# Decay gates as one stacked product, tokens that begin at 128 bytes, and mixing in the wide PSUM bank

## The chip, the cores and the metric

The kernel runs on one core of one Trainium2 chip. Its time is the device time of one execution in microseconds (us); the median of several runs counts. A profile shows one execution, taken by the hardware profiler. Engines: TensorE (PE; its weight loads PEld), VectorE (DVE), ScalarE (ACT), GpSimd (POOL) and SyncE (SP), which issues the DMAs.

## The reference

One block of a streaming encoder on 1024 tokens and 16 meta tokens in front of them, width 1024, all in float32. A normed input is projected into eight parts. One branch takes trailing means over 2, 4, 8 and 16 positions and mixes them; the other is gated linear attention in chunks of 64, whose decays come from a product of rank 16; both are merged by gates. A squared-ReLU MLP of width 4096 follows. Cut to what the change touches:

```python
z = jnp.einsum('bld,dn->bln', u, w_in)
a, q, k, v, r, lr, ga, gb = jnp.split(z, IN_SPLITS, axis=-1)     # lr: 16 columns
p = multiscale_pool(a).reshape(B, L, POOL_GROUPS, POOL_GROUP_DIM)
p = jnp.einsum('blgc,gce->blge', p, w_pool_mix).reshape(B, L, POOL_WIDTH) * pool_scale
...
log_a = jax.nn.log_sigmoid((lr @ w_gate_up + b_gate).astype(jnp.float32)) / GLA_TAU
...
o = gla_chunked(q, k, v, log_a)
```

## The kernel before

Nearly every matrix product is made from operands split in two: `hi` is the value rounded to float32r by a ScalarE copy, `lo` the rest by a VectorE subtraction, and a product is three float32r matmuls, hi·hi + hi·lo + lo·hi (`mm3`, lines 280 to 282). The tokens live transposed, features on the partitions, in four tiles: `TH[0]`, `TL[0]` for the first 512 tokens and `TH[1]`, `TL[1]` for the rest, each with 8 blocks (k) of 128 features. The first half's rows hold 528 numbers: the 16 meta tokens, then the 512 tokens, which so begin at number 16, or byte 64 (`OFF`, line 208). The second half's rows hold 512.

The stages, in the order of TensorE's program:

- `start` (line 431): for each tile of 128 tokens the norm, the transposes into `TH`/`TL` (`transposed`, lines 266, 222, 223), and the value projections with the tokens as the stationary operand (`v_tile`, line 390). The first group's value weights carry 16 more columns, the rank-16 input `lr` (272 columns in place of 256). At its end `lr_turn` (line 412) transposes `lr` into `lrT_meta` and into the first 16 partitions of `gB`, by nine transposes and three ScalarE copies. The gate weights `wgu` (16 rows of 256) are loaded there as well (line 502).
- Pooling, gates and keys: `pool_open` (line 539) gives the room of `start` back and makes the buffers; then the steps of the list in line 631 follow: four pooling blocks `a_block`, two decay steps `decays`, four mixing steps `mix_block`, and the two key blocks `k_block`, in the order a0, gate 0, a1, gate 1, mix 0, a2, mix 1, a3, mix 2, k0, mix 3, differences, k1. A pooling or key block projects all 1040 tokens in three pieces (`WITH_META`, line 285): 264 + 264 columns of the first half with the meta tokens, and 512 of the second; 24 matmuls each.
- A decay step (`log_decay`, line 511) makes two products of 512 tokens and one of the 16 meta tokens, each as one float32 matmul over 16 rows with `wgu` as weights (line 514); then a chain of five ScalarE and one VectorE instructions makes log-sigmoid and the decay of each half (lines 515 to 519, 528).
- A mixing step (line 568) makes the window sums on VectorE, splits them into `ph`, and multiplies each half by the group's mixing weights. Before, the first half's product goes to a bank of the pool `ms`, which the gates and transposes use too, and the second half's to `sc`, one tile of two banks whose halves `bank("sc")` gives out in turn (line 154).
- The pairs of projections (line 764): the other projections as 11 pairs of blocks, each by seven products of half size. Products P1 and P2 (bank `sc`) take `TH[0]`/`TL[0]` as the moving operand, P5 and P3 (bank `z`) `TH[1]`/`TL[1]`, and P6, P7, P4 (bank `y`) sums of tokens in tiles of their own. Each product is a group of twelve matmuls of 512 columns. The attention inside the chunks is interleaved.
- Attention across the chunks, output projection, and the MLP by the same seven products. There P1 and P2 read `TH[0]`/`TL[0]` through views with rows of 512 numbers from the tile's beginning (`MH`, `ML`, line 210).

TensorE's order is the program's. The instructions of the other engines and the DMAs, which SyncE issues, are put in order by the scheduler from their dependencies and a cost model, and each engine works off its list in order. Weights come through two staging buffers (`Raw`) and the ring `W1` of two slots, split at lines 84 and 85. Storage on chip is two stacks, `left` and `right`; a tile pushed where another lay waits for that one's last use.

Of the kernel before, what the change touches and what calls it, by code (L numbers as in the profile page):

```python
# [7 lines left out]
F32 = mybir.dt.float32  # L8
# [19 lines left out]
C_A, C_Q, C_K, C_V, C_R, C_LR, C_GA, C_GB = 0, 512, 768, 1024, 1536, 2048, 2064, 3088  # L28
VP = 272
NPAIR = DFF // P // 2  # L30
MP = 264
PACE, LEVEL, OPENING, STRETCH = 1.3, 1.6, 6.0, 1.9


# [88 lines left out]
def kernel(  # L123
# [71 lines left out]
    stat = [tiny(16) for _ in range(4)]  # L195
    eps_t = tiny(1)
    pool.memset(eps_t, EPS)
    wgu = left.push("wgu", [16, 256], F32)
    metab = left.push("metab", [P, 5, 16], F32)
    lrT_meta = left.push("lrT_meta", [16, META], F32)  # L200
    raw = Raw(nc, [left.push(f"raw{i}", [P, D], F32) for i in range(2)])
    W1 = Ring(tc, raw, left.push("w1h", [P, 2, D], F32R), left.push("w1l", [P, 2, D], F32R), 2)
    left_ff = left.mark()
    TH, TL = [], []
    for h, n in ((0, HALF + META), (1, HALF)):
        TH.append(left.push(f"th{h}", [P, KT, n], F32R))
        TL.append(left.push(f"tl{h}", [P, KT, n], F32R))
    OFF = (META, 0)

    MH, ML = ([a.rearrange("p k c -> p (k c)")[:, : KT * HALF].rearrange("p (k c) -> p k c", k=KT) for a in t] for t in (TH, TL))  # L210

# [69 lines left out]
            pe.matmul(ps, ah, bl, start=False, stop=False, skip_group_check=more)  # L281
            pe.matmul(ps, al, bh, start=False, stop=last and i == n - 1, skip_group_check=more)  # L282

    MAIN = [(0, META, HALF), (1, 0, HALF)]
    WITH_META = [(0, 0, MP), (0, MP, MP), (1, 0, HALF)]

    def project(wb, pieces, evac, kt=KT, free=True, src=None):
        xh, xl = src or (TH, TL)
# [101 lines left out]
    def v_tile(i, t):  # L390

        vw, w = S["vw"][i], 256 + 16 * (i == 0)
        if t == 8:
            half, at, n = 0, 0, META
        else:
            half, n = t // 4, P
            at = OFF[half] + (t % 4) * P
        b = bank("mm")[:n, :w]
        mm3(
            b, KT, lambda k: (TH[half][:, k, at : at + n], TL[half][:, k, at : at + n]),  # L400
            lambda k: (vw[:, 0, k], vw[:, 1, k]),
        )
        if i == 0:
            dve.tensor_copy(S["lrtok"][:n, t], b[:, 256:])
        if t == 8:
            act.activation(vm[:, i * 256 : i * 256 + 256], b[:, :256], ACT.Copy)
        else:
            o = nxt("vo")
            act.activation(o, b[:, :256], ACT.Copy)
            nc.sync.dma_start(v_dram[i, t], o)  # L410

    def lr_turn():
        b = bank("ms")
        pe.transpose(b[:16, :16], S["lrtok"][:16, 8], ident[:16, :16])
        act.activation(lrT_meta, b[:16, :16], ACT.Copy)
        for h in range(2):
            b = bank("ms")
            for t in range(4):
                pe.transpose(b[:16, t * P : (t + 1) * P], S["lrtok"][:, 4 * h + t], ident)
            act.activation(gB[:16, h * HALF : (h + 1) * HALF], b[:16], ACT.Copy)  # L420


    SPREAD = {
# [7 lines left out]
    def start():  # L431
        act.preload_act_table_set("natural_log_exp_and_others")
        xs = left.push("xs", [P, 4, D], F32)
        us = left.push("us", [P, 3, D], F32)
        S["lrtok"] = left.push("lrtok", [P, 10, 16], F32)
        S["lrraw"] = left.push("lrraw", [P, KT, 16], F32)
        xm = left.push("xm", [META, D], F32)
        um = left.push("um", [META, D], F32)
        mf = left.push("mf", [P, 6, CH], F32)
        S["xr"] = right.push("xr", [P, KT, SEQ], F32)  # L440
        S["vw"] = [right.push(f"vw{i}", [P, 2, KT, n], F32R) for i, n in enumerate((VP, 256))]
        buffer("vo", 3, 2 * P, right)
        load = lambda t: nc.sync.dma_start(xs[:, t % 4], x[t * P : (t + 1) * P, :])
        blank = S["xr"].rearrange("p k c -> p (k c)")[:, -640:]
        pool.memset(blank, 0.0)

        def warm(n, cols=HALF):
            for _ in range(n):
                pe.matmul(bank("ms")[:, :cols], blank[:, HALF:], blank[:, :cols], start=True, stop=True)

        load(0)
        nc.sync.dma_start(um[:1], norm_mix[None, :])
        nc.sync.dma_start(ident, ident_in)
        ask_vw(0)
        nc.sync.dma_start(S["lrraw"], w_in[:, C_LR : C_LR + 16].rearrange("(k p) c -> p k c", p=P))
        pool.memset(xm[:1, :P], 1.0)
        warm(2)
        for c in halves():
            b = bank("mm")
            pe.matmul(b, xm[:1, :P], um[:1, c], start=True, stop=True)  # L460
            dve.tensor_copy(gB[:, c], b)
        warm(2)
        for t in range(8):
            if 0 < t < 6:
                load(t + 2)
            if t == 1:
                nc.sync.dma_start(xm, meta)
            if t == 3:
                W1.top_up()
            u = us[:, t % 3]  # L470
            layer_norm(xs[:, t % 4], u)
            transposed(u, t // 4, OFF[t // 4] + (t % 4) * P, ("ms", "sc"))
            if t == 0:
                load(1)
                load(2)
                warm(10, P)
                load_vw(0)
                ask_vw(1)
            if t == 6:
                layer_norm(xm, um)  # L480
            if t == 1:
                warm(6, P)
            if t == 2:
                load_vw(1)
            if t < 3:
                v_tile(0, t)
            else:
                for i, n in SPREAD[t]:
                    v_tile(i, n)
        transposed(um, 0, 0)  # L490
        v_tile(0, 7)
        v_tile(1, 6)
        v_tile(1, 7)
        v_tile(0, 8)
        v_tile(1, 8)
        lr_turn()
        nc.sync.dma_start(mf, masks)
        pool.tensor_copy(mask, mf)
        nc.sync.dma_start(pscale, col(pool_scale, 4))
        nc.sync.dma_start(bgate, col(b_gate, 2))  # L500
        nc.sync.dma_start(gnorm, col(gla_norm, 4))
        nc.sync.dma_start(wgu, w_gate_up)

    one = []
    step(one, start)
# [5 lines left out]
    def log_decay(lrT, p, n, y, t):  # L511

        b = bank("ms")[:, :n]
        pe.matmul(b, wgu[:, p * P : (p + 1) * P], lrT, start=True, stop=True)
        act.activation(y, b, ACT.Identity, bias=bgate[:, p : p + 1])
        act.activation(t, y, ACT.Abs)
        act.activation(t, t, ACT.Exp, scale=-1.0)
        act.activation(t, t, ACT.Ln, bias=1.0)
        dve.scalar_tensor_tensor(y, y, 0.0, t, ALU.min, ALU.subtract)
# [3 lines left out]
    def decays(p):  # L523
        def fn():
            for half, c in enumerate(halves()):
                y = nxt("c")
                log_decay(gB[:16, c], p, HALF, y, nxt("t1"))
                act.activation(y, y, ACT.Exp, scale=1.0 / TAU)
                nc.sync.dma_start(decay_dram[p, half], y)
                yield 0.6  # L530
            if p:
                act.activation(gnorm, gnorm, ACT.Copy, scale=0.5)
            log_decay(lrT_meta, p, META, metab[:, META_LOG[p]], metab[:, 4])
            if p:
                tc.keep_in_program_order(act.preload_act_table_set("exp_and_others"))

        return fn

    def pool_open():
        left.pop_to(base)  # L540
        right.pop_to(1)
        buffer("c", 4)
        buffer("t1", 3)
        S["left_t"] = left.mark()
        buffer("a", 2, 1056)
        buffer("s", 2, 1056)
        S["ph"] = left.push("ph", [P, 2, SEQ], F32R)
        mw = S["mw"] = left.push("mw", [P, 2, 4, P], F32R)
        r = raw.load(w_pool_mix.rearrange("g c e -> c g e"), 4 * P).rearrange("p (g e) -> p g e", g=4)
        act.activation(mw[:, 0], r, ACT.Copy)  # L550
        dve.tensor_tensor(mw[:, 1], r, f32(mw[:, 0]), ALU.subtract)
# [5 lines left out]
    def a_block(g):  # L557
        def fn(wb):
            a = pooled[g] = nxt("a")

            def evac(b, half, at, n):
                c = at if half == 0 else META + HALF
                act.activation(a[:, c : c + n], b, ACT.Copy)

            yield from project(wb, WITH_META, evac)

        return fn

    def mix_block(g):
        def fn():  # L570
# [10 lines left out]
            for c in halves():  # L581
                act.activation(S["ph"][:, 0, c], pp[:, c], ACT.Copy)
                dve.tensor_tensor(S["ph"][:, 1, c], pp[:, c], f32(S["ph"][:, 0, c]), ALU.subtract)
            for h, (tag, c) in enumerate(zip(("ms", "sc"), halves())):
                b = bank(tag)
                mm3(b, 1, lambda i: wb, lambda i: (S["ph"][:, 0, c], S["ph"][:, 1, c]))
                o = nxt("c")
                act.activation(o, b, ACT.Copy, scale=pscale[:, g : g + 1])
                nc.sync.dma_start(pm_dram[g, h], o)
                yield  # L590
# [3 lines left out]
    def k_block(p):  # L594
        def evac(b, half, at, n):
            o = nxt("c")[:, :n]
            act.activation(o, b, ACT.Copy)
            c = at if half == 0 else META + HALF
            nc.sync.dma_start(k_dram[p, :, c : c + n], o)

        return lambda wb: project(wb, WITH_META, evac)
# [1029 lines left out]
```

## Time and profile before

| | |
|---|---|
| median of 3 runs | 1226.18 us |
| the runs | 1226.18, 1223.92, 1226.18 us |
| profiled execution | 1222.42 us |
| its span, first to last instruction | 1220.6 us |
| mean granted TensorE clock | 0.999 |
| matmuls in the span | 6807 |

In the rows of a timeline stand start and length in us, the engine, the line, the operation and `out<-in` with shapes and a count; instructions of one kind that follow each other are merged into one row. A bracket at the end is the engine's idle time before the row and who ended it. In the table of stages stand the stretch, its length, and then for each engine its busy time with the number of instructions, in the order PE, PEld, DVE, ACT, POOL; then the granted clock, the share of the DMA engines and GB/s.

### The profile page before, as it was taken

What the parts mean: (1) busy time and instruction counts of PE and PEld (TensorE: products, weight loads), DVE (VectorE), ACT (ScalarE), POOL (GpSimd) and SP (SyncE); (2) the same over time, 40 slices, a digit from 0 to 9 for tenths busy, and PEclk for the clock granted to TensorE, in tenths of its full rate; (3) what the DMA queues carried; (4) which work ended last, traced back from release to release, by engine and by line L of the source; (5) the groups of instructions that cost most, each with busy time, mean ns of one, the idle gap of its engine ahead of it and who ended that gap; (6) DMA issues with size and microseconds to landing.
All of it is one profiled execution on the core that took longest, in us unless ns stands there. A gap on an engine that the chain in (4) does not pass through costs nothing.

```text
span 1220.6 us, 18363 instructions
## 1 busy us (share of the span) xinstructions
PE 1204.6 (99%) x6807; PEld 996.5 (82%) x6807; DVE 838.9 (69%) x1381; ACT 572.3 (47%) x1009; POOL 75.7 (6%) x96
## 2 busy tenths in 40 slices
PE   9999999999999999999999999999999999999997
PEld 7988977777778887888778888888888888888886
DVE  7536557565777569735887677676775887887686
ACT  8536444444456224314655455454554444444544
POOL 0000053322230000000000000000000000000000
PEclk9999999999999999999999999999999999999999
DMA  8213334435338967821244454444569973333532
GB/s 261 73 35 114 104 95 137 141 104 166 96 121 291 326 222 248 296 67 69 104 139 156 143 162 152 148 155 145 173 228 322 334 246 104 96 95 96 171 96 87
DMA packets 153355, 192.76 MB, mean 158 GB/s; under 512 B 12177, under 2 KB 88225, under 8 KB 153266
## 3 DMA queue, kind: packets, MB, share of 16 engines
q1 hardware_dynamic: 153266, 191.59, 48.9%
q8 instruction: 53, 0.87, 0.3%
q14 instruction: 36, 0.29, 0.1%
HBM read 128.62 MB, written 62.93 MB: 157 GB/s over the span
## 4 chain that ended last, share of the span: by engine, by line
PE 89%; DVE 4%; DMA 3%; ACT 1%; issue 1%; POOL 0%; SPq 0%; DVEq 0%; ACTq 0%; POOLq 0%
PE b_mm L280 7%; PE b_mm L282 7%; PE b_mm L281 7%; PE b_y L280 6%; PE b_y L282 6%; PE b_y L281 6%; PE b_oa L281 5%; PE b_oa L282 5%; PE b_oa L280 5%; PE b_z L280 4%; PE b_z L282 4%; PE b_z L281 4%; PE b_sc L280 4%; PE b_ob L281 4%; PE b_ob L282 4%; PE b_ob L280 4%
## 5 line engine op out<-in xcount | busy, mean ns | idle before, releaser
L685 ACT ACTIVATE w1h<-raw 128x512 fp32r<-128x512 f32 x106 | 65.9, 623 | 57.9 <-PE b_y L281 25.3
L686 DVE TENSOR_TENSOR w1l<-raw,w1h 128x512 fp32r<-128x512 f32 x106 | 72.5, 685 | 20.5 <-ACT w1h L685 20.5
L280 PE MATMUL b_sc<-th,w1h 128*128 128x512 f32 x216 | 85.7, 397 | 0.7 <-ACT u2p L1414 0.7
L280 PE MATMUL b_z<-th,w1h 128*128 128x512 f32 x216 | 85.3, 395 | 0.6 <-DVE c L804 0.4
L281 PE MATMUL b_sc<-tl,w1h 128*128 128x512 f32 x216 | 84.9, 393 | 0.0
L281 PE MATMUL b_z<-tl,w1h 128*128 128x512 f32 x216 | 84.3, 391 | 0.4 <-DVE tl L1300 0.4
L282 PE MATMUL b_sc<-th,w1l 128*128 128x512 f32 x216 | 84.5, 391 | 0.0
L685 ACT ACTIVATE w1h<-fs 128x512 fp32r<-128x512 f32 x81 | 51.1, 631 | 71.1 <-PE b_y L281 33.2
L282 PE MATMUL b_z<-th,w1l 128*128 128x512 f32 x216 | 84.2, 390 | 0.0
L686 DVE TENSOR_TENSOR w1l<-fs,w1h 128x512 fp32r<-128x512 f32 x81 | 56.9, 702 | 25.9 <-ACT w1h L685 25.8
L280 PE MATMUL b_mm<-th,w1h 128*128 128x512 f32 (+1 forms) x208 | 72.2, 347 | 0.0
L281 PE MATMUL b_mm<-tl,w1h 128*128 128x512 f32 (+1 forms) x208 | 71.1, 342 | 0.0
L282 PE MATMUL b_mm<-th,w1l 128*128 128x512 f32 (+1 forms) x208 | 71.1, 342 | 0.0
L685 ACT ACTIVATE w1h<-bt 128x512 fp32r<-128x512 f32 x46 | 29.1, 632 | 70.9 <-issue 43.9
L1490 DVE TENSOR_TENSOR bt<-w,w 128x512 f32<-128x512 f32 x80 | 54.7, 684 | 0.7 <-DMA w<-in_w_ff_dram 0.6
L280 PE MATMUL b_mm<-wo,th 128*128 128x512 f32 x128 | 50.4, 394 | 0.0
L282 PE MATMUL b_mm<-wo,tl 128*128 128x512 f32 x128 | 50.0, 390 | 0.0
L281 PE MATMUL b_mm<-wo,th 128*128 128x512 f32 x128 | 49.9, 390 | 0.0
L280 PE MATMUL b_y<-wo,w1h 128*128 128x512 f32 x128 | 49.9, 389 | 0.0
L282 PE MATMUL b_y<-wo,w1l 128*128 128x512 f32 x128 | 49.8, 389 | 0.0
L281 PE MATMUL b_y<-wo,w1h 128*128 128x512 f32 x128 | 49.8, 389 | 0.0
L686 DVE TENSOR_TENSOR w1l<-bt,w1h 128x512 fp32r<-128x512 f32 x46 | 31.8, 691 | 25.6 <-ACT w1h L685 25.6
(405 smaller groups left out, 3331.8 us busy)
## 6 DMA issues: line engine op xcount, KB each, us to landing
hf_dram<-h SPq DMA_DIRECT2D x112, 256.0 KB, 2.1
raw<-hf_dram SPq DMA_DIRECT2D x112, 256.0 KB, 2.6
w<-in_w_ff_dram SPq DMA_DIRECT2D x64, 256.0 KB, 4.7
raw<-in_w_in_dram SPq DMA_DIRECT2D x22, 512.0 KB, 4.7
raw<-in_w_ff_dram SPq DMA_DIRECT2D x16, 512.0 KB, 4.2
rawx<-in_w_ff_dram SPq DMA_DIRECT2D x16, 512.0 KB, 4.3
rawp<-in_w_in_dram SPq DMA_DIRECT2D x10, 512.0 KB, 4.3
xs<-in_x_dram SPq DMA_DIRECT2D x8, 512.0 KB, 4.9
```

The costliest lines, as they stand in the source:

```text
L280: pe.matmul(ps, ah, bh, start=first and i == 0, stop=False, skip_group_check=more)
L281: pe.matmul(ps, ah, bl, start=False, stop=False, skip_group_check=more)
L282: pe.matmul(ps, al, bh, start=False, stop=last and i == n - 1, skip_group_check=more)
L685: act.activation(hi, a, ACT.Copy)
L686: dve.tensor_tensor(lo, a, f32(hi), ALU.subtract)
L1490: dve.tensor_tensor(bt, w, S["w2"][q[3:]][:, i], ALU.add if q[2] == "+" else ALU.subtract)
```

## The change

It has three parts.

1. The decay gates. `lr` goes into a tile of 96 partitions that is cleared first: rounded values in rows 0 to 15 and again in rows 64 to 79, the rest (`lo`) in rows 32 to 47. The gate weights are loaded three times into a tile with the same rows: rounded in rows 0 to 15 and 32 to 47, the rest in rows 64 to 79. One float32r matmul over 96 rows then sums hi·hi + lo·hi + hi·lo. `lr_turn` moves from the end of `start` to the beginning of `pool_open`, behind the point where the room of the value weights is given back, since the new tiles lie there.
2. The first half's rows grow from 528 to 544 numbers. Meta tokens stand at 16 to 31, the tokens begin at 32, or byte 128. A block's pieces of the first half are 272 + 256 columns in place of 264 + 264.
3. Mixing uses the two halves of `sc` for both products.

```diff
-MP = 264
+LEAD = 32
...
-    wgu = left.push("wgu", [16, 256], F32)
-    metab = left.push("metab", [P, 5, 16], F32)
-    lrT_meta = left.push("lrT_meta", [16, META], F32)
+    metab = left.push("metab", [P, 6, 16], F32)
...
-    for h, n in ((0, HALF + META), (1, HALF)):
+    for h, n in ((0, HALF + LEAD), (1, HALF)):
...
-    OFF = (META, 0)
+    OFF = (LEAD, 0)
...
-    WITH_META = [(0, 0, MP), (0, MP, MP), (1, 0, HALF)]
+    WITH_META = [(0, LEAD - META, 272), (0, LEAD + 256, 256), (1, 0, HALF)]
...
     def lr_turn():
+        def stacked(to, b):
+            act.activation(to[:16], b, ACT.Copy)
+            act.activation(to[64:80], b, ACT.Copy)
+            dve.tensor_tensor(to[32:48], b, f32(to[:16]), ALU.subtract)
+
         b = bank("ms")
         pe.transpose(b[:16, :16], S["lrtok"][:16, 8], ident[:16, :16])
-        act.activation(lrT_meta, b[:16, :16], ACT.Copy)
-        for h in range(2):
+        stacked(S["lr"][:, SEQ : SEQ + META], b[:16, :16])
+        for h, c in enumerate(halves()):
             b = bank("ms")
             for t in range(4):
                 pe.transpose(b[:16, t * P : (t + 1) * P], S["lrtok"][:, 4 * h + t], ident)
-            act.activation(gB[:16, h * HALF : (h + 1) * HALF], b[:16], ACT.Copy)
+            stacked(S["lr"][:, c], b[:16])
...
-        lr_turn()
...
-        nc.sync.dma_start(wgu, w_gate_up)
...
-        pe.matmul(b, wgu[:, p * P : (p + 1) * P], lrT, start=True, stop=True)
+        pe.matmul(b, S["gu"][:, p * P : (p + 1) * P], lrT, start=True, stop=True)
...
-                log_decay(gB[:16, c], p, HALF, y, nxt("t1"))
+                log_decay(S["lr"][:, c], p, HALF, y, nxt("t1"))
...
     def pool_open():
+        right.pop_to(1)
+        S["lr"] = right.push("lr", [96, SEQ + 2 * META], F32R)
+        S["gu"] = right.push("gu", [96, 256], F32R)
+        wgu = right.push("wgu", [96, 256], F32)
+        pool.memset(f32(S["lr"]), 0.0)
+        pool.memset(wgu, 0.0)
+        for r in (0, 32, 64):
+            nc.sync.dma_start(wgu[r : r + 16], w_gate_up)
+        lr_turn()
+        act.activation(S["gu"], wgu, ACT.Copy)
+        dve.tensor_tensor(S["gu"][64:96], wgu[64:], f32(S["gu"][64:96]), ALU.subtract)
         left.pop_to(base)
-        right.pop_to(1)
...
-            for h, (tag, c) in enumerate(zip(("ms", "sc"), halves())):
+            for h, (tag, c) in enumerate(zip(("sc", "sc"), halves())):
```

The other lines change with these: the meta tokens' place in `v_tile` and in the call of `transposed`, and the column at which a piece's result is put.

More of the change, by code (lines that the diff above doesn't have):

```diff
@@ L282, in mm3 @@
             pe.matmul(ps, al, bh, start=False, stop=last and i == n - 1, skip_group_check=more)
-    MAIN = [(0, META, HALF), (1, 0, HALF)]
-    WITH_META = [(0, 0, MP), (0, MP, MP), (1, 0, HALF)]
+    WITH_META = [(0, LEAD - META, 272), (0, LEAD + 256, 256), (1, 0, HALF)]
     def project(wb, pieces, evac, kt=KT, free=True, src=None):
@@ L393, in v_tile @@
         if t == 8:
-            half, at, n = 0, 0, META
+            half, at, n = 0, LEAD - META, META
         else:
@@ L489, in start @@
                     v_tile(i, n)
-        transposed(um, 0, 0)
+        transposed(um, 0, LEAD - META)
         v_tile(0, 7)
@@ L532, in fn @@
                 act.activation(gnorm, gnorm, ACT.Copy, scale=0.5)
-            log_decay(lrT_meta, p, META, metab[:, META_LOG[p]], metab[:, 4])
+            log_decay(S["lr"][:, SEQ : SEQ + META], p, META, metab[:, META_LOG[p]], metab[:, 4])
             if p:
@@ L561, in evac @@
             def evac(b, half, at, n):
-                c = at if half == 0 else META + HALF
+                c = at - LEAD + META if half == 0 else META + HALF
                 act.activation(a[:, c : c + n], b, ACT.Copy)
@@ L597, in evac @@
             act.activation(o, b, ACT.Copy)
-            c = at if half == 0 else META + HALF
+            c = at - LEAD + META if half == 0 else META + HALF
             nc.sync.dma_start(k_dram[p, :, c : c + n], o)
```

## The prediction

> **What bounds the kernel now.** I read the page first, then the table of stages, then TensorE's timeline around the lines that the diff touches. The page's busy times and the shares of its chain:
>
> ```profile
> PE 1204.6 (99%) x6807; PEld 996.5 (82%) x6807; DVE 838.9 (69%) x1381; ACT 572.3 (47%) x1009; POOL 75.7 (6%) x96
> ...
> PE 89%; DVE 4%; DMA 3%; ACT 1%; issue 1%; POOL 0%; SPq 0%; DVEq 0%; ACTq 0%; POOLq 0%
> ```
>
> TensorE is busy 99% of the span and carries 89% of the chain that ended last, so what it is given to do sets the time. A share over the whole kernel is not enough: the two stages that the diff touches have to be full themselves. In the table of stages the first number behind the stage's length is TensorE's busy time:
>
> ```profile
> 76.00:156.00 80.00, 80.00 (x486) 70.13 (x484) 41.83 (x56) 44.11 (x79) 0.00 (x0) 1.00 0.29 90
> 156.00:386.00 230.00, 229.56 (x1797) 181.20 (x1796) 154.19 (x245) 105.95 (x178) 74.18 (x88) 1.00 0.45 139
> ```
>
> From 76 to 156 us (pooling and key blocks, decay gates, mixing) TensorE has no idle time; from 156 to 386 us (the pairs of projections) 0.44 us in 230. VectorE and ScalarE have half of the first stage free. So a microsecond of TensorE work taken out there should come off the end, unless a wait takes its place.
>
> **The gates.** The two decay steps on TensorE's timeline, each with its two products of 512 columns (four rows merged into one), the meta product of 16 columns, and the first matmul behind them:
>
> ```profile
> 88.77 1.98 PE L514 MATMUL b_ms<-gB,wgu 16*128 16x512 f32 x4
> 90.59 0.29 PE L514 MATMUL b_ms<-lrT_meta,wgu 16*128 16x16 f32 x2
> 90.80 0.39 PE L280 MATMUL b_mm<-th,w1h 128*128 128x264 f32 x1
> ...
> 102.34 1.98 PE L514 MATMUL b_ms<-gB,wgu 16*128 16x512 f32 x4
> 104.16 0.29 PE L514 MATMUL b_ms<-lrT_meta,wgu 16*128 16x16 f32 x2
> 104.44 0.47 PE L280 MATMUL b_ms<-ph,mw 128*128 128x512 f32 x1
> ```
>
> Pace is read from start to start, since the ends of matmuls are modelled. Two float32 products take 90.59 − 88.77 = 1.82 us, 0.91 us each. The steps take 90.80 − 88.77 = 2.03 us and 104.44 − 102.34 = 2.10 us. The change makes of each product one float32r matmul over 96 rows. What such a one costs, stands in the pairs (next fence): twelve of 512 columns in 2.72 us, 0.227 us each, a quarter of 0.91. Rows shouldn't matter: the float32 product used 16 of 128, and still needs four times the time. The 16-column product costs 0.21 us in its float32 form (two instructions); as one instruction it is between nothing and 0.21, and I take half, 0.10. A step is then 2 × 0.227 + 0.10 = 0.55 us, and the gates save (2.03 − 0.55) + (2.10 − 0.55) = 3.0 us, with 0.2 either way for the small product.
>
> **The 128-byte start.** TH[0] and TL[0] are the first half's tokens. Before, a row is 528 numbers (2112 bytes) and tokens begin 64 bytes in; after, 544 numbers (2176 bytes) and 128. They are the moving operand of P1 and P2 (b_sc) in the pairs. First matmuls of three successive groups of twelve; then of two in the squared-ReLU stage, where b_sc reads the same tiles through rows of 2048 bytes with no lead (each row from a stretch of its own):
>
> ```profile
> 219.79 0.39 PE L280 MATMUL b_y<-t2h,w1h 128*128 128x512 f32 x1
> 222.51 0.40 PE L280 MATMUL b_sc<-th,w1h 128*128 128x512 f32 x1
> 225.32 0.40 PE L280 MATMUL b_z<-th,w1h 128*128 128x512 f32 x1
> 701.39 0.39 PE L280 MATMUL b_sc<-th,w1h 128*128 128x512 f32 x1
> 704.12 0.39 PE L280 MATMUL b_z<-th,w1h 128*128 128x512 f32 x1
> ```
>
> A b_y group takes 222.51 − 219.79 = 2.72 us, the b_sc group 225.32 − 222.51 = 2.81 us, and in the later stage a b_sc group 704.12 − 701.39 = 2.73 us. Bank and weight ring are alike; what differs is where the moving rows lie. The excess is 0.08 to 0.09 us, and there are 11 pairs with two such groups: 22 × 0.08 = 1.8 us. The trace can't say whether the start or the row length does it, since both differ between the slow case and the fast one; after the change the start is mended and rows are still not 2048 bytes. I take the whole 1.8, as all fast rows start on 128 bytes; the ends are 0 and 2.0.
> The Trainium skill, page "SBUF — State Buffer", section Specifications (TRN2), gives SBUF lines of 16 bytes. By that rule 64 and 128 are equally good starts, and this term would be nothing; the row at 222.51 speaks against it so far, and the case is the first rival below.
>
> Against that stands the cutting of the 528 columns into 272 + 256 where it was 264 + 264, in six blocks (four pooling, two key). Two value tiles of 272 and 256 columns, up to the last matmul of the second; then the start of two 264-column pieces and of the piece behind (stretches of their own again):
>
> ```profile
> 48.18 0.37 PE L280 MATMUL b_mm<-vw,th 128*128 128x272 f32 x1
> 51.29 0.28 PE L280 MATMUL b_mm<-vw,th 128*128 128x256 f32 x1
> 54.05 0.28 PE L282 MATMUL b_mm<-vw,tl 128*128 128x256 f32 x1
> 118.57 0.28 PE L280 MATMUL b_mm<-th,w1h 128*128 128x264 f32 x1
> 121.47 0.29 PE L280 MATMUL b_mm<-th,w1h 128*128 128x264 f32 x1
> 124.41 0.39 PE L280 MATMUL b_mm<-th,w1h 128*128 128x512 f32 x1
> ```
>
> 264 + 264 takes 124.41 − 118.57 = 5.84 us. The value tiles give 51.29 − 48.18 = 3.11 us for 272, and 2.76 us for 23 spacings of 256, so 2.88 for 24: 5.99 together. Six blocks lose at most 6 × 0.15 = 0.9 us; by columns they lose nothing. The nearest rows are the 264s (same tiles, same weights), so I take 0.2.
>
> **The moved rank-16 turn and its new operand.** On TensorE nothing moves: the nine transposes stand behind the last value tile both times. What is new is in front of the first gate product. Rows that price it:
>
> ```profile
> 73.39 0.29 PE L282 MATMUL b_mm<-vw,tl 128*16 128x272 f32 x1
> 0.77 0.63 POOL L445 MEMSET xr<- 128x640 f32 x1
> small<-in_b_gate_dram SPq DMA_DIRECT2D x1, 1.0 KB, 2.4
> 74.83 16.54 SPq L118 DMA_DIRECT2D raw<-in_w_in_dram  x2
> 78.80 1.05 ACT L420 ACTIVATE gB<-b_ms 16x512 f32<-16x512 f32 x2
> ```
>
> The stacked tiles lie where the first value weights lay, which are last read at 73.39. GpSimd then clears 1056 and 256 columns: by 0.63 us for 640, 1.3 us, to about 75.0 (GpSimd has nothing else before 156, where its column reads 0.00). SyncE issues three loads of the gate weights where there was one, early and unhindered; a small load lands in 2.4 us, so about 78.5 with three issues. ScalarE copies 256 columns and VectorE subtracts, under 1 us. Beside that ScalarE has two copies for each half where it had one (four times 0.52 us by the row at 78.80, 1.05 more) and VectorE three subtractions. All is done by about 83, and the product is wanted at 88.77: 5 to 6 us of cover, so I cost it at nothing. If the cover is gone it costs what is late, for behind a gate product that waits stands all of TensorE's list.
>
> **Mixing in the wide bank.** Both halves of a group now use the two columns of `sc`; no matmul more or less, and nothing has to wait for a gate bank to be emptied. What is next in line when the gates are short:
>
> ```profile
> 102.22 1.06 ACT L84 ACTIVATE w1h<-raw 128x1024 fp32r<-128x1024 f32 x1 [2.38 <-PE b_mm L281]
> ...
> 108.23 0.68 ACT L588 ACTIVATE c<-b_ms,small 128x512 f32<-128x512 f32 x1
> ...
> 112.70 1.16 ACT L582 ACTIVATE ph<-s 128x512 fp32r<-128x512 f32 x2
> ...
> 118.62 0.68 ACT L588 ACTIVATE c<-b_ms,small 128x512 f32<-128x512 f32 x1
> 113.37 1.29 DVE L583 TENSOR_TENSOR ph<-s,ph 128x512 fp32r<-128x512 f32 x2 [1.29 <-ACT ph L582]
> 117.89 0.39 PE L280 MATMUL b_sc<-ph,mw 128*128 128x512 f32 x1
> ```
>
> The second group's mixing starts 0.68 us (three matmuls) before 117.89, at 117.21, and needs `ph`, done at 113.37 + 1.29 = 114.66. TensorE comes there 3.0 us sooner, at 114.2. ScalarE's run towards `ph` starts at 102.22, released by the block between the two gate steps, and so moves 1.5 us with the first of them: `ph` at 113.2. One microsecond is left; no wait, but this is the thinnest place.
>
> **Sum.** −3.0 − 1.8 + 0.2 = −4.6 us. The profiled execution took 1222.42 us (span 1220.6 and 1.8 around it), so 1217.8 by its own measure. The median of the three runs before is 1226.18, 3.8 above that execution, and by the median the forecast is 1221.6.
>
> **The rivals.**
> *The start buys nothing* (row length is what counts, or 16-byte lines): the gates alone, −3.0 + 0.2 = −2.8 us, 1223.4. For it: rows remain off 2048 bytes, and the 264-column pieces begin at all sorts of places without a visible price. Against it: every fast moving row starts on 128 bytes.
> *The gate weights come late.* SyncE's list is served in order, and between its issues at 74.83 and the end of that merged row (91.4) it waits for a staging buffer. If the three loads are listed behind that second load, they issue until 92.4, land at 94.8, and with 0.8 us of copying the first gate product starts at 95.6 where it would at 88.77: 6.8 us lost, −4.6 + 6.8 = +2.2, 1228.4. Against it: they can go at 75, long before that load can.
> *The two halves of the wide bank are tied (slower).* Each mixing group would wait with its second product until ScalarE has read the first. For the first group TensorE has its first product done at about 102, while ScalarE's list reaches that reading at 108.23, done at 108.91, 1.5 us sooner with its run: 107.4, a wait of 5.3. For the second the reading ends at 118.62 + 0.68 = 119.30, where the second product stood at 117.89: 1.4, and likewise for two more. 5.3 + 3 × 1.4 = 9.5 us, −4.6 + 9.5 = +4.9, 1231.1. It decides from 4.6 us of such waits on. Against it: the halves are separate banks of 512 columns. The trace before never has both in use by one group, so it can't exclude it.
>
> **How the numbers follow.** A measurement of this kernel can tell 0.2%, 2.5 us, from no change. Forecast 0.64; start without effect 0.20; late weights or other waits that give the gain back 0.09; tied halves 0.07. The forecast lies beyond 2.5 us; the first rival lies at its edge, and I give half of its chance to each side; 0.04 of the forecast's goes to small waits that bring it under 2.5, and 0.01 of the late weights' to a wait some tenths longer than worked out. Faster 0.60 + 0.10 = 0.70, same 0.04 + 0.10 + 0.08 = 0.22, slower 0.07 + 0.01 = 0.08. The range goes from 1217.2 (both savings at their upper ends, −3.2 − 2.0, on the profiled execution, should the runs after fall that low) up to 1225.5: the gates with the 0.9 us of the 272s (1224.1) and 1.4 us of waits. That leaves out the tied halves and most of the late weights.
>
> **What would show it.** Right: the decay steps take 0.5 to 0.6 us from start to start; b_sc groups take 2.72 to 2.73 us in the pairs; TensorE's column from 76 to the end of the key blocks still equals the stage, which is some 3 us shorter. Wrong: TensorE waits for `lr`, `gu` or `ph` (the gates' cover or the thin place has failed), an idle time before the second product of a mixing group (tied halves), or b_sc groups still at 2.81 us (start without effect). All of it is wrong if the two stages are 4.6 us shorter and later stages as much longer.

## The result and the profile after

The changed kernel takes 1234.49 us (median of 6 runs, 1233.25 to 1237.07), the kernel before, run beside it, 1226.18 (6 runs, 1223.92 to 1226.63): a ratio of 1.0076, 95% interval 1.0062 to 1.0090. It is slower by 8.3 us by the medians, 9.3 by the ratio, where 4.6 us less were forecast. The profiled execution has a span of 1231.4 us, 10.7 above that of before.

Busy times and the shares of the chain, from the page of after; then the stage from 76 to 156 us, the first number behind its length being TensorE's busy time:

```profile
PE 1205.9 (98%) x6801; PEld 997.3 (81%) x6801; DVE 840.6 (68%) x1385; ACT 574.2 (47%) x1013; POOL 77.3 (6%) x98
...
PE 80%; DVE 4%; DMA 1%; ACT 1%; issue 1%; DVEq 0%; ACTq 0%; SPq 0%
```

```profile
76.00:156.00 80.00, 71.38 (x434) 63.40 (x433) 40.33 (x58) 42.51 (x78) 0.00 (x0) 0.96 0.29 87
```

TensorE's share of the chain that ended last fell from 89% to 80%. The stage from 76 to 156 us, full before, now has 8.6 us in which TensorE stands idle, and its mean granted clock is 0.96 where it was 1.00. TensorE's own view of waits between 95 and 160 us has one entry for its products (us in total, times, longest):

```profile
PE b_sc L278 <- ACT c L598: 8.6, 4, 5.1
```

Four waits of the mixing's product for ScalarE's reading of the other column of `sc`, one in each group: the prediction's third rival. TensorE's timeline shows the two decay steps and the first mixing group, and behind it ScalarE's reading:

```profile
89.00 0.65 PE L514 MATMUL b_ms<-lr,gu 96*128 96x512 f32 x3
89.50 0.37 PE L278 MATMUL b_mm<-th,w1h 128*128 128x272 f32 x1
...
100.90 0.65 PE L514 MATMUL b_ms<-lr,gu 96*128 96x512 f32 x3
101.41 0.48 PE L278 MATMUL b_sc<-ph,mw 128*128 128x512 f32 x1
...
107.48 0.80 PE L278 MATMUL b_sc<-ph,mw 128*128 128x512 f32 x1 [5.13 <-ACT c L598]
108.07 0.63 PE L279 MATMUL b_sc<-ph,mw 128*128 128x512 f32 x1
108.50 0.63 PE L280 MATMUL b_sc<-ph,mw 128*128 128x512 f32 x1
```

```profile
106.73 0.70 ACT L598 ACTIVATE c<-b_sc,small 128x512 f32<-128x512 f32 x1
```

The decay steps take 0.50 and 0.51 us from start to start where they took 2.03 and 2.10: 3.1 us are saved. But the first mixing product stands right behind them, ScalarE is still working through the gates' activations, and reads its bank only at 106.73. The reading ends at 107.43, and at 107.48 the second product starts, 6.07 us behind the first (0.76 before: 104.44 in the prediction's rows, and 105.20 below). The other three groups have 2.15, 2.15 and 1.72 us from product to product where they had 0.68. Together that is 5.31 + 1.47 + 1.48 + 1.04 = 9.30 us. Three rows for the comparison, each from a stretch of its own: the first group's second product and the second group's first, both before the change, and the second group's first after it:

```profile
105.20 0.39 PE L280 MATMUL b_sc<-ph,mw 128*128 128x512 f32 x1
117.21 0.39 PE L280 MATMUL b_ms<-ph,mw 128*128 128x512 f32 x1
121.48 0.39 PE L278 MATMUL b_sc<-ph,mw 128*128 128x512 f32 x1
```

The windows behind the long wait (the number before the DMA share is the granted clock):

```profile
104.00:110.00 6.00, 2.52 (x8) 2.23 (x9) 4.94 (x11) 5.98 (x14) 0.00 (x0) 0.57 0.56 172
110.00:120.00 10.00, 10.00 (x63) 9.32 (x62) 1.85 (x6) 2.65 (x6) 0.00 (x0) 0.92 0.15 56
```

After the pause the clock is granted at half: the products at 108.07 and 108.50 are 0.43 us apart, where 0.227 is the rule. From the second product to the next group's first, 107.48 to 121.48, it takes 14.0 us; before, the same block took 12.0 (105.20 to 117.21). So the pause costs 2.0 us more than its own length.

From the first mixing product to the first group of the pairs the kernel thus loses 9.3 + 2.0 + 0.3 = 11.6 us, having gained 3.3 on the way from the turn of the rank-16 rows to that product. Two later stretches, from the pairs' first group with `t0h` to the scores (the first product into `b_gs`) and from there to the first product with `wo`, are 1.3 and 0.9 us longer, and the start of the profiled execution 0.3. Over all profiles of the whole block in this study these two stretches lie between 25.4 and 26.9 and between 308.3 and 311.3 us with no order by version, so I put nothing of them down to the change.

For the second stretch the traces show a cause. TensorE waits 2.3 us for weights in it, at 484 us after and at 475 us before, and behind that wait the clock was granted at half after the change and in full before it:

```profile
487.15:490.56 3.41, 2.95 (x8) 2.03 (x7) 2.71 (x4) 0.67 (x2) 0.00 (x0) 0.50 0.95 344
474.00:480.00 6.00, 3.08 (x13) 1.93 (x12) 5.57 (x9) 2.50 (x4) 0.00 (x0) 1.00 0.94 301
```

The same wait stands in all twelve profiles of the block. In nine of them the half clock follows it, for 3.41 us, or once 6.83. From the first product with `yg`, in front of the wait, to the first with `wo` it is 43.9 us in the three with the full clock, 44.9 to 45.5 in eight and 46.7 in the one. The half clock there comes and goes whatever the version; what it hangs on is taken up under "The pause filled".

### The profile page after: what moved, and what is told of

Read it like the earlier page. It is cut to its first block, busy times and chain, and to the rows that moved or that the text cites. A ratio compares the mean times of both kernels' runs of the same rounds, so it can differ in the third digit from the quotient of the medians.

```text
span 1231.4 us, 18373 instructions
## 1 busy us (share of the span) xinstructions
PE 1205.9 (98%) x6801; PEld 997.3 (81%) x6801; DVE 840.6 (68%) x1385; ACT 574.2 (47%) x1013; POOL 77.3 (6%) x98
## 4 chain that ended last, share of the span: by engine, by line
PE 80%; DVE 4%; DMA 1%; ACT 1%; issue 1%; DVEq 0%; ACTq 0%; SPq 0%
PE b_y L278 6%; PE b_y L280 6%; PE b_y L279 6%; PE b_oa L280 5%; PE b_oa L278 5%; PE b_oa L279 5%; PE b_mm L278 4%; PE b_mm L280 4%; PE b_mm L279 4%; PE b_z L278 4%; PE b_z L279 4%; PE b_z L280 4%; PE b_sc L278 4%; PE b_sc L279 4%; PE b_sc L280 4%; PE b_ob L280 4%
## 5 line engine op out<-in xcount | busy, mean ns | idle before, releaser
L278 PE MATMUL b_mm<-th,w1h 128*128 128x512 f32 (+2 forms) x208 | 72.6, 349 | 0.0
L279 PE MATMUL b_mm<-tl,w1h 128*128 128x512 f32 (+2 forms) x208 | 71.7, 345 | 0.0
L280 PE MATMUL b_mm<-th,w1l 128*128 128x512 f32 (+2 forms) x208 | 71.6, 344 | 0.0
L695 ACT ACTIVATE w1h<-bt 128x512 fp32r<-128x512 f32 x46 | 29.1, 632 | 70.8 <-issue 43.9
L278 PEld LDWEIGHTS b_sc<-th,w1h 128*128 128x128 f32 x216 | 40.5, 188 | 11.5 <-ACT u2p L806 1.4
```

Of the source, the lines that this page charges most:

```text
L278: pe.matmul(ps, ah, bh, start=first and i == 0, stop=False, skip_group_check=more)
L695: act.activation(hi, a, ACT.Copy)
```

## The experiments

All ratios are to the kernel before, run beside on the same chip.

**Part 3 alone: the mixing in the wide bank, on the kernel before.**

```diff
-            for h, (tag, c) in enumerate(zip(("ms", "sc"), halves())):
+            for h, (tag, c) in enumerate(zip(("sc", "sc"), halves())):
```

> The kernel before with part 3 alone (both mixing products in the wide bank). Theory A: four waits; the first product of the first group is done at 105.2 and its reading ends at 108.9, so 3.7 us, then 1.4 three times: 7.9 us, and up to 2 us of halved clock if 3.7 us is enough for that: 1234.1 to 1236.1, ratio 1.006 to 1.008. Theory B gives the same here. If the waits come from the shortened gates, none: 1226.2.

Measured: 1235.55 us, ratio 1.0080 (1.0065 to 1.0095). Its waits between 95 and 170 us, and the windows from 104 to 120:

```profile
PE b_sc L280 <- ACT c L588: 7.1, 4, 3.6
```

```profile
104.00:110.00 6.00, 4.01 (x14) 2.08 (x12) 3.95 (x4) 5.09 (x9) 0.00 (x0) 0.92 0.22 56
110.00:120.00 10.00, 8.38 (x50) 8.09 (x51) 4.89 (x14) 6.32 (x14) 0.00 (x0) 0.71 0.35 126
```

This one line carries the whole loss, with the same four waits. The longest is 3.6 us, since the gates still take their full time ahead of it, and there too the half clock comes.

**Parts 1 and 2: part 3 undone in the changed kernel** (the same line the other way round).

> The changed kernel with the first half's mixing back in the gates' pool, the second half's in the wide bank (part 3 alone undone). Theory A (the second product of a mixing group waits until ScalarE has read the first, 9.3 us in four waits, and the clock is halved for a while after the longest, 2.0 us; the gates save 3.3): no such wait, no stretch below full clock; but the first mixing product now comes just behind the gates and wants the bank of their first product, which ScalarE reads at about 102.3 to 103.0, so one wait of 1.0 to 1.6 us. 1226.2 - 3.3 + 1.3 = 1224.2, ratio to before 0.998. Theory B (the new layout of the first half costs 2.2 us in the pairs and behind them, whatever the waits): the same waits gone, but 1226.4, ratio 1.000.

Measured: 1224.09 us, ratio 0.9990 (0.9981 to 1.0000). One wait is left in the mixing:

```profile
PE b_ms L278 <- ACT c L515: 1.5, 1, 1.5
```

The first mixing product waits for a gate bank. That is what the wide bank was to take away, and it eats half of the gates' 3.1 us. The measured ratio lies between the two that were expected, 0.998 and 1.000, so theory B (2.2 us for the new layout) isn't decided here; the versions at 64 and at 128 bytes below, which differ by that layout alone and can't be told apart in time, speak against it.

**Part 1 alone: the gates on the kernel before** (tokens at 64 bytes, pieces of 264, mixing in `ms` and `sc`).

> The kernel before with the new gates alone: tokens at byte 64, pieces of 264 + 264, mixing in the gates' pool and the wide bank. Theory A: as the kernel with part 3 undone, within 0.5 us: 1224.2, ratio 0.998, with the same one wait at the first mixing product; a value tile of the first half 0.03 us shorter. Theory B: 2 us below that kernel.

Measured: 1223.27 us, ratio 0.9983 (0.9971 to 0.9994), with the same wait of 1.5 us. It can't be told from the run before it: the two intervals overlap from 0.9981 to 0.9994.

**Both products first.** The wide bank is kept, but a group issues both products ahead of both readings:

```diff
-            for h, (tag, c) in enumerate(zip(("sc", "sc"), halves())):
-                b = bank(tag)
+            bs = [bank("sc") for _ in range(2)]
+            for b, c in zip(bs, halves()):
                 mm3(b, 1, lambda i: wb, lambda i: (S["ph"][:, 0, c], S["ph"][:, 1, c]))
+            for h, b in enumerate(bs):
                 o = nxt("c")
```

> The changed kernel, but each mixing group issues both products before either is read; the banks are as in the change. Theory A, with the tie made by the program's order (the second product is listed behind a reading of the same two-bank tile, and the tile is guarded as one): no waits, full clock, 1226.2 - 3.3 = 1222.9, ratio 0.997; the reading of the first half starts only behind the second product. Rival (the two halves of the wide bank can't be used side by side whatever the order, or the wait is for the reading of the group before): waits of 1 to 5 us remain and it stays above 1230. Theory B: no waits, and 1225.1, ratio 0.999.

Measured: 1221.32 us, ratio 0.9969 (0.9956 to 0.9982); no wait in the mixing and the full clock. The first group:

```profile
103.77 0.48 PE L278 MATMUL b_sc<-ph,mw 128*128 128x512 f32 x1
...
104.55 0.40 PE L278 MATMUL b_sc<-ph,mw 128*128 128x512 f32 x1
```

0.78 us from product to product, as before the change. The banks, their number and the work are those of the changed kernel; only the order in which products and readings are written differs. So it is the order that ties the halves. The code gives the reason: both columns of `sc` are one tile of the program, and a product that is written behind a reading of that tile waits for it, though it is in the other column.

**The pause filled.** The changed kernel with TensorE kept busy between the two products of the first group:

```diff
+                if g == 0 and h == 0:
+                    idle = bank("ms")
+                    for _ in range(18):
+                        pe.matmul(idle, wb[0], S["ph"][:, 0, c], start=True, stop=True)
```

> The changed kernel with one addition: between the two products of the first pooling group, while TensorE would stand idle, 18 products of 512 columns run into a bank of their own that nobody reads (about 18 x 0.227 = 4.1 us). Theory A (the pause of 5.1 us is one loss, the half clock granted behind it a second one): the first reading and the second product stay where they are (some 6 us from product to product), the granted clock stays full from 104 to 120 us, the next stretch of projections goes from 14.0 us back to 12.0, and the time from 1234.5 to about 1232.4. Rival (the low clock is not caused by the idle stretch, or costs nothing): clock and stretch as in the changed kernel, 1234.5.

Measured: 1232.54 us, ratio 1.0060 (1.0046 to 1.0074). The second product and the windows behind it:

```profile
107.09 0.50 PE L278 MATMUL b_sc<-ph,mw 128*128 128x512 f32 x1
```

```profile
104.00:110.00 6.00, 5.95 (x34) 4.95 (x33) 4.90 (x12) 5.97 (x14) 0.00 (x0) 1.00 0.66 215
110.00:120.00 10.00, 10.00 (x60) 8.63 (x58) 1.53 (x4) 2.98 (x6) 0.00 (x0) 1.00 0.07 26
```

The second product comes no sooner (6.08 us behind the first), but the clock stays full, and the next group's first product follows in 12.1 us, not 14.0. The ratio falls from 1.0076 to 1.0060, 2.0 us of 1226; the two intervals overlap, so it is the trace of the block, 14.0 against 12.1 us, that shows this, and the times only agree with it. So the half clock is a second cost, caused by the idle time.
The Trainium skill, page "TensorE: Matmul & The Clock Gate", Part 1, says that the clock falls to half after an idle window of about 3.4 us, counted by a free-running window. The traces agree with the window: in each profile the changes of the clock lie whole multiples of 3.413 us apart (104.86, 111.69, 487.15 and 490.56 us after the change). They don't agree that the window has to be idle throughout. Leave out the first 16 us of each execution and its end. In the stretches of 3.413 us that ended with a fall to half, TensorE stood idle for 1.9 to 2.6 us; in those at full clock that ended without one, for 1.8 us at most, the waits of 0.9 to 1.5 us among them. So it matters how a wait lies to the grid: that of 2.3 us falls whole into the stretch from 483.74 to 487.15 after the change, and before it the grid parts it at 476.57 into 1.8 and 0.5. One fall, in "part 3 alone", stands out with 1.0 us of idle time, in a stretch that also holds float32 products of 16 rows, and what brought it stays open.

**The pace of the rows by itself.** A kernel without the block: groups of twelve products of 512 columns from rows laid as before (64 bytes, 2112 long), as after (128, 2176), and with no lead (2048), first alone and then with ScalarE and VectorE copying.

> No block at all: 48 groups of 12 products of 512 columns, 16 each from rows that begin at 64 bytes with a row of 2112 bytes (as before), at 128 bytes with 2176 (as after), and at 0 with 2048, first with every other engine idle, then again with ScalarE and VectorE copying all the time; the output is not the block's. Spacing from the first to the last product of a group is read. Theory S (where a row begins sets the pace): 2.575, 2.54 and 2.493 us, with and without company. Theory C (the pace of those groups comes from what other engines do beside them): 2.493 for all three alone, and the same higher figure for all three in company.

Measured in one profiled run: the windows go from the start of one group to the start of the thirteenth behind it; 156 weight loads are thirteen times twelve.

```profile
46.96:83.10 36.14, 36.14 (x158) 29.30 (x156) 0.00 (x0) 0.00 (x0) 0.00 (x0) 1.00 0.00 0
91.45:127.67 36.22, 36.22 (x157) 29.25 (x156) 0.00 (x0) 0.00 (x0) 0.00 (x0) 1.00 0.00 1
135.92:171.28 35.36, 35.36 (x157) 29.28 (x156) 0.00 (x0) 0.00 (x0) 0.00 (x0) 1.00 0.00 0
179.59:215.72 36.13, 36.13 (x157) 29.30 (x156) 36.13 (x61) 36.13 (x71) 0.00 (x0) 1.00 0.00 1
224.07:260.30 36.23, 36.23 (x158) 29.25 (x156) 36.23 (x61) 36.23 (x71) 0.00 (x0) 1.00 0.00 1
```

By thirteen that is 2.780 us from group to group at 64 bytes, 2.786 at 128 and 2.720 without lead; with the other engines at work 2.779 and 2.787. Company does nothing, so theory C is out, and 128 bytes are no better than 64, where theory S had them 0.035 us better.

**Starts and row lengths.** The same with 21 pairs of start and row.

> No block again: groups of 12 products of 512 columns as in the run before, from one buffer each for the two terms, ten groups for each of 21 pairs of start and row length, nothing else at work; the output is not the block's. Spacing of groups is read. Rows of 2048 bytes with starts at 0, 16, 32, 64, 128, 256, 512 and 1024 bytes, the same operand for all products with starts 0, 64 and 128, and rows of 2112, 2176, 2304, 2560 and 3072 bytes with starts at 0 and with a lead. Theory S (the start, below some multiple): at rows of 2048 bytes starts that are no multiple of it take 2.780 us or more from group to group, the others 2.720, and rows of 2304 or more are quick once start and row are multiples of it. Theory R (the row): at rows of 2048 bytes every start takes 2.720, and every other row 2.78, whatever the start.

Measured in one profiled run, starts counted from the beginning of the buffer: windows over six groups; rows of 2048 bytes with starts at 0, 16, 32, 64, 128 and 256, then a row of 2304 with start 0.

```profile
18.05:34.37 16.32, 16.32 (x73) 13.51 (x72) 0.00 (x0) 0.00 (x0) 0.00 (x0) 1.00 0.00 1
45.43:62.11 16.68, 16.68 (x74) 13.54 (x72) 0.00 (x0) 0.00 (x0) 0.00 (x0) 1.00 0.00 1
73.29:90.09 16.80, 16.80 (x73) 13.49 (x72) 0.00 (x0) 0.00 (x0) 0.00 (x0) 1.00 0.00 1
101.13:117.61 16.48, 16.48 (x73) 13.52 (x72) 0.00 (x0) 0.00 (x0) 0.00 (x0) 1.00 0.00 1
128.72:145.45 16.73, 16.73 (x73) 13.56 (x72) 0.00 (x0) 0.00 (x0) 0.00 (x0) 1.00 0.00 1
156.43:172.75 16.32, 16.32 (x74) 13.51 (x73) 0.00 (x0) 0.00 (x0) 0.00 (x0) 1.00 0.00 0
...
431.91:448.23 16.32, 16.32 (x73) 13.52 (x72) 0.00 (x0) 0.00 (x0) 0.00 (x0) 1.00 0.01 1
```

A sixth of each is 2.720, 2.780, 2.800, 2.747, 2.788, 2.720 and 2.720 us. Of the 21 pairs, the eleven in which all starts are multiples of 256 bytes take 2.720, whatever the row (2048, 2304, 2560 or 3072, or one row for all products); the ten others take 2.747 to 2.800, those of before and after among them. Theory S holds, with 256 bytes for its multiple, but for its size at a start of 64 bytes: 2.747 where 2.780 or more was expected. In the rows of after every other row begins on a multiple of 256 (2176 is 8.5 times that), and the pace is no better for it.

**Tokens at 64 bytes against 128 bytes**, both with the mended mixing, on one chip.

> The changed kernel with both products of a pooling group issued ahead of both readings, and with the first half's tokens back at 64 bytes (pieces 264 + 264): parts 1 and 3 of the change, mended, without part 2. My forecast of part 2 (-1.8 + 0.2) would make this 1.6 us slower than the version at 128 bytes beside it. Theory now (the start gives about 0.3 us in the feed-forward groups and costs 0.25 in the value tiles): no difference, both about 1221.3, within 0.6.

> The same with the tokens at 128 bytes, once more, on the same chip as the version at 64 bytes: 1221.3, ratio to before 0.996 to 0.998.

Measured: 1223.31 us, ratio 0.9979 (0.9968 to 0.9990), at 64 bytes; 1222.78, 0.9985 (0.9975 to 0.9996), at 128. No difference can be told. The second is the kernel "both products first" once more, and came out at the upper end of what it had been (0.9969): the two intervals overlap from 0.9975 to 0.9982.

**Tokens at 256 bytes.** `LEAD = 64`, a buffer (`u2p`) opened later to make room, mixing mended; and a version whose rows begin with the tokens and end with the meta tokens.

> The changed kernel with both products of a pooling group issued ahead of both readings and the first half's tokens at 256 bytes of rows of 2304 bytes (LEAD 64; the place for it comes from opening a buffer of the feed-forward stage later). Theory S with 256 bytes for the multiple (from the run on starts and rows: 2.720 us from group to group against 2.787 at 128 bytes and 2.780 at 64): the 22 groups of the feed-forward pairs that read these rows go from 2.541 to 2.493 us, those behind them from 2.525 to 2.493, 22 x 0.067 = 1.5 us less than at 128 bytes: about 1221.3, ratio to before 0.9965. Rival (other engines' work, or what stands beside the rows, sets the pace there): groups stay at 2.54, ratio 0.9977 as without it.

> The same with the tokens at the very start of rows of 2304 bytes and the meta tokens behind them (pieces 256 + 272; the pooling's and the keys' readings of the second piece are split in two, which adds an ACTIVATE and a store to each). Theory S: the same 1.5 us in the pairs, and the pieces of the projections with the first half, both on multiples of 256 bytes now, a little shorter too (5.87 us for the two at 128 bytes; perhaps 0.1 less in each of six blocks): 0.5 us under the version at 256 bytes. Rival: the two added readings of each block cost more than that, ScalarE being the releaser of the mixing: same or slower than it.

Measured: 1224.27 us, ratio 0.9994 (0.9983 to 1.0005), and 1225.24, 0.9999 (0.9987 to 1.0011). The groups of the pairs had the quick pace in both, and yet the time was lost: the last stage (from its first product to the end of its last), 304.8 us in all profiles so far, took 308.9 in both. The second version isn't the 0.5 us quicker that theory S had; the two can't be told apart. It begins with waits that the others don't have (waits from 900 us on, first version):

```profile
PE b_oa L279 <- DVE fxl L697: 1.0, 1, 1.0
PE b_oa L278 <- ACT fxh L696: 0.9, 1, 0.9
```

and the granted clock is 0.96 from 910 to 950 us: half of it for 3.41 us behind these two waits. `fxh` and `fxl` are buffers of that stage, which now lay over others, since I had opened `u2p` elsewhere. My edit for the room, not the start, had cost 4.1 us. So once more with `u2p` put above the operands of the stage:

> The version at 256 bytes once more, with the late buffer put above the operands of the feed-forward stage and not beneath them, since the first one lost 4.1 us where the last stage begins (304.8 to 308.9 us from its first product to the end), in a place that has nothing to do with the start of the rows. If those 4.1 us came from which buffers the last stage's first ones lie over, the last stage is back at 304.8, the groups stay at 2.493, and the time is 0.8 to 1.0 us below the version at 128 bytes: ratio to before about 0.997. If they came from the rows at 256 bytes, 308.9 stays, and the ratio is 0.999 to 1.000 as before.

Measured: 1222.78 us beside 1226.49 of before, ratio 0.9964 (0.9953 to 0.9976), and the last stage is back at 304.8. Groups of the pairs in its trace, as quoted for after in the next section:

```profile
219.72 0.39 PE L278 MATMUL b_y<-t2h,w1h 128*128 128x512 f32 x1
222.44 0.39 PE L278 MATMUL b_sc<-th,w1h 128*128 128x512 f32 x1
225.16 0.39 PE L278 MATMUL b_z<-th,w1h 128*128 128x512 f32 x1
227.88 0.39 PE L278 MATMUL b_y<-t0h,w1h 128*128 128x512 f32 x1
```

Three times 2.72 us. This is the best ratio of the study, 4.4 us under before by the ratio and 3.7 by the medians. Its interval overlaps that of the mended mixing alone, so that the whole time is better for the 256 bytes isn't shown; that the groups are, is. From the first to the last `b_sc` group of the pairs it is 220.8 to 221.1 us in the three profiles at 256 bytes and 221.0 to 222.4 in the nine others, and the two overlap. But the stretch up to the scores that varies by itself (25.4 to 26.9 us) lies in there, with three of the 22 groups. Without it, it is 194.7 us in the three profiles at 256 bytes, 195.6 to 195.7 in the five at 128 and 195.8 in the four at 64: 1.1 us won by 256 bytes and 0.1 to 0.3 by 128.

## Why the prediction was wrong, point by point

**The step that failed** is "Mixing in the wide bank", which the sum put at nothing: "no matmul more or less, and nothing has to wait for a gate bank to be emptied". So much is so: no product waited for a gate bank. But four products had to wait for the reading of the other column of `sc`, 9.3 us together, and the longest wait brought 2.0 us of half clock. The prediction had the mechanism as its third rival, priced at 5.3 us for the first wait and 1.4 for each of the others (measured: 5.31, 1.47, 1.48 and 1.04) and at 1231.1 for the time, and gave it 0.07. What was held against it, that the halves are separate banks of 512 columns, is not the point: the code opens `sc` as one tile and hands out its columns, so the order of products and readings was to be checked line by line. The trace of before could not show it, as no group there used both columns. Experiments "part 3 alone" and "both products first" settle it: the line alone costs 9.8 us (1226 × 0.0080), and the order alone takes all of it away.

**The half clock** was in none of the cases. Of the 12.9 us between the forecast (1221.6) and the result, the waits are 9.3 and the clock 2.0; the missing gain of the start, below, is 1.5 to 1.7.

**The gates** were right: steps of 0.50 and 0.51 us where 0.55 was worked out, 3.1 us saved where 3.0 was forecast. What the sum put no price on is that a gate step which ends sooner meets gate banks that are not empty yet, though the prediction names them. With `ms` in the mixing that is a wait of 1.5 us (experiments "parts 1 and 2" and "part 1 alone"); so part 3, in the right order, is worth those 1.5 us in the traces.

**The 128-byte start** was mis-sized: 1.8 us forecast, 0.1 to 0.3 measured. Successive groups of the pairs after the change, and last, from before, the group behind the prediction's 222.51 and 225.32:

```profile
229.62 0.39 PE L278 MATMUL b_y<-t2h,w1h 128*128 128x512 f32 x1
232.34 0.40 PE L278 MATMUL b_sc<-th,w1h 128*128 128x512 f32 x1
235.12 0.40 PE L278 MATMUL b_z<-th,w1h 128*128 128x512 f32 x1
237.87 0.39 PE L278 MATMUL b_y<-t0h,w1h 128*128 128x512 f32 x1
228.05 0.39 PE L280 MATMUL b_y<-t0h,w1h 128*128 128x512 f32 x1
```

The `b_sc` group went from 2.81 to 2.78 us, but the one behind it from 2.73 to 2.75: 5.527 for the two where 5.534 was measured before, 22 × 0.007 = 0.15 us by these groups, and 0.1 to 0.3 by the stretch of the pairs above (195.8 to 195.6 or 195.7). The reading that the start sets the pace was right, and so was the excess of 0.08 that it was taken from; that 128 bytes are enough was a guess, because the quick rows happened to begin on multiples of 256 and so of 128 too. At 256 bytes the two groups take 5.440, 0.094 less than before. That times 22 would be 2.1 us, and the stretch above gives 1.1 for 19 of them: counting all 22 alike was a second error of this term. In the traces 13 of the `b_sc` groups become 0.08 us shorter, but the eight right behind products of the attention (`b_gs`) only 0.04; one varies by itself. On this term the first rival ("the start buys nothing") came true but for 0.1 to 0.3 us.
It gave as one reason the 16-byte lines of the Trainium skill, page "SBUF — State Buffer", section Specifications (TRN2). The runs speak against starts on 16 bytes being equal for the moving operand: 2.780 at 16 and 2.720 at 0.

**The pieces** of 272 and 256 cost next to nothing (each row from a stretch of its own):

```profile
124.43 0.29 PE L278 MATMUL b_mm<-th,w1h 128*128 128x272 f32 x1
127.43 0.28 PE L278 MATMUL b_mm<-th,w1h 128*128 128x256 f32 x1
130.28 0.40 PE L278 MATMUL b_mm<-th,w1h 128*128 128x512 f32 x1
```

5.85 us for the two, 5.84 before; the forecast of 0.2 for six blocks and its ends hold. Not in the sum was that the same rows are the stationary operand of the value tiles: a tile of 256 columns went from 2.73 to 2.76 us from its first product to its last, 0.2 to 0.3 us for the eight tiles of the first half.

**The moved turn** was right: the last of the new operand (`gu`) was done at 83.6 us and wanted at 89.0, 5.4 us of cover where 5 to 6 were forecast, and no wait for `lr` or `gu` appeared. Nor did TensorE wait for `ph`, the thin place.

## What to carry to other kernels

Where two halves of a tile are used in turn, write both producers ahead of both readers, and check this in the code whenever a bank is exchanged: a trace in which the halves were never used together says nothing of it. A pause of TensorE is to be priced with the half clock that may stand behind it: here 2.0 us on a wait of 5.1, and even a wait of 2.3 us brought it in nine of twelve profiles, while single waits of 1.5 us and less did not. And an engine that becomes faster runs into the next buffer that is not empty: a saving is worth what the next wait leaves of it, here 1.6 of 3.1 us until the bank was changed in the right order.

## What was not expected of the hardware

Start-to-start time of products of 512 columns depends on where the moving rows begin: 0.2267 us at multiples of 256 bytes, and 0.229 to 0.233 in the mean at 16, 32, 64 or 128 bytes beside, not in the order of the distance (64 is the best of these, 32 the worst). Where only a group's own rows are off, the group behind it pays a part: 2.75 us in place of 2.72 at 128 bytes, 2.73 at 64. What in the reading of a row makes this isn't settled by these runs. Whether the memory would let a product into one column of `sc` while ScalarE reads the other was not tried either, as it would need the program's order taken away.
